# A two-layer hybrid backbone on one core: head 0's keys loaded early, transposes over two PSUM pools, and the last projection as seven block products

## The chip, the cores and the metric

The kernel runs on one core of a Trainium2 chip. Its engines work in parallel, each through its own list of instructions in order: TensorE (PE) multiplies matrices and writes to PSUM, VectorE (DVE) and ScalarE (ACT) work on tiles element by element, GpSimd (POOL) does so more slowly, and SyncE (SP) issues the transfers between HBM and SBUF. They wait for each other by semaphores. The metric is the device time of one execution in microseconds (us), as the median of three runs; lower is better.

## The reference

There are 512 latent tokens x, 256 context tokens and a width of 2048. Layer 1 is even, layer 2 odd; both have adaLN (shift, scale and gate from the conditioning) ahead of them and a gated residual behind. Cut to what matters here:

```python
def even_layer(...):                       # layer 1
    h = modulate(rms_norm(x, norm_g), sh, sc)
    au, av, ag, bq, bk, bv, bg = split(h @ w_in)
    q, k = diff_qk(bq, ...), diff_qk(bk, ...)      # QK-norm and rotary; keys of ctx appended
    ob = blocked_diff_attention(q, k_all, v_all, lam)   # 8 heads, two maps each
    y = even_branch_out(au, av, ag, ob, bg, ...)
    return x + gt * (y @ w_out)

def conv_module(h, w_in, dw_w, dw_b, ln_g, ln_b):   # in layer 2
    a, b, g = jnp.split(h @ w_in, 3, axis=-1)
    y = a * jax.nn.sigmoid(b)
    y = depthwise_conv_31(y) + dw_b
    y = jax.nn.silu(layer_norm(y, ln_g, ln_b))
    return y * jax.nn.silu(g)

def odd_layer(...):
    h = modulate(rms_norm(x, norm_g), sh, sc)
    return x + gt * (conv_module(h, ...) @ w_out)
```

Everything is float32. The last product, `conv_module(...) @ w_out` in layer 2, is 512x2048 by 2048x2048.

## The kernel before

**Arithmetic.** A float32 product is made of three matmuls on parts of reduced width: each operand is split in a rounded part (hi) and the rest (lo), and hi·hi, lo·hi and hi·lo are added up in PSUM. For weights, `load_w` (lines 97 to 105) loads a raw tile of 128 x 2048 elements (four blocks of 128 rows by 512 columns, 1 MB), ACT copies it to `whi` (L103) and DVE or POOL subtracts to get `wlo` (L104). Raw tiles have three buffers, `whi` and `wlo` two each. Activations are split the same way by `split` (L111 on ACT, L112 on DVE).

**Stages.** By the profiled execution's clock: adaLN and the keys of the context to about 140 us; layer 1's input projections and the gated MLP to 648; attention, filled up with the remaining projections, to 970; its output projection and the residual to 1131; h2, layer 2's modulated input, transposed by PE and split, to 1191; layer 2's input projection, in groups of four 128-column tiles with DVE running the 31-tap convolution beside it, to 1673; the last projection to 1847.

**Order.** In the input projections of layer 1 and in attention, PE and SP follow the order of the code (a manual schedule). Elsewhere the scheduler of the tile framework sets each engine's order from its own estimates and from priorities: weight loads and their splits are put 100 places ahead (`W_AHEAD`), the gates' work 600 (`E_AHEAD`). Within an engine the resulting order is fixed: an instruction that waits holds up all behind it.

**The places that the change touches.** `load_kq` (L828 to 835) loads the keys `kk` and queries `qq` of a head from HBM into the attention's pool, which has two buffers for each; head 0 is loaded right at the attention's start, with `S` (the scores) waiting for it. `make_h2` transposes four 128x128 blocks into one PSUM tile of the pool `psM` (two banks, `z4`), from which ACT (L1061) and DVE (L1062) make h2's hi and lo. The other six banks belong to `psA` (`mt`). At the end of layer 2 the chain `ln_chain` normalises the 16 conv tiles `zs` (16 tiles of the pool `rs4`, tag `res`), multiplies by the gates `sg` (pool `sg4`; L1167 makes a gate from its projection `tg`), and `y2_split` makes hi and lo. The chain's pieces are taken between the granules of the last three gate projections, so most of it comes after the mean and variance of all conv tiles are known. The last projection then runs over four groups of 512 columns (`og`) with four loads of 512 rows each (`gi`): a granule is one load and 48 matmuls of 512 columns, into four banks. Its `wlo` is made on POOL. After each group DVE multiplies by the gate (L1244), adds x1 (L1245), and SP writes the output.

## Time and profile before

| | us |
|---|---|
| three runs | 1850.75, 1850.77, 1851.95 |
| median | 1850.77 |
| the profiled execution's own time | 1853.68 |
| its span (first to last instruction) | 1851.9 |
| PE busy | 1805.9 (98%), 8767 instructions |
| DVE busy | 1122.3 (61%) |
| ACT busy | 559.8 (30%) |
| POOL busy | 446.9 (24%) |
| mean granted clock of TensorE | 0.996 |

A row of the profile's groups reads: line, engine, operation, output from inputs, shapes, how many; then busy time and mean ns of one; then the engine's idle time before them and what ended it. A row of the timeline reads: start, duration, engine, line, operation, how many in a row, and in brackets how long the engine had been idle and what released it. A row of the windows: stretch, length, busy time (with instructions) of PE, its weight loads, DVE, ACT and POOL, the granted clock, the DMA engines' busy share and GB/s. A row of the waits: engine, line, what it waited for, total us, times, longest.

### The profile page before, as it was taken

The numbers are of one execution on the slowest core, as the hardware profiler recorded it, in microseconds if no ns is written. First come the engines' busy times: TensorE is split into PE (matmuls) and PEld (weight loads), VectorE is DVE, ScalarE is ACT, GpSimd is POOL, SyncE is SP. The second block draws the span as 40 slices with busy tenths as digits, with TensorE's granted clock in tenths as the row PEclk, the third lists the DMA queues.
The fourth block names the chain that finished last, engine by engine and source line by source line (L and its number), as shares of the span: only waits on it lengthen the run. The fifth ranks groups of instructions, "written<-read, shape, count | busy, mean of one in ns | idle before, by whom it ended". The sixth has DMA issues, their size and how long they took to land.

```text
span 1851.9 us, 21931 instructions
## 1 busy us (share of the span) xinstructions
PE 1805.9 (98%) x8767; PEld 1475.8 (80%) x8767; DVE 1122.3 (61%) x1571; ACT 559.8 (30%) x747; POOL 446.9 (24%) x173
## 2 busy tenths in 40 slices
PE   5899999999999989999999999999999999999998
PEld 2557888888878878888888889888888888888887
DVE  4438546288556336666674555149999999765111
ACT  3322212222323124444442225322222222464120
POOL 0002002011000032232310002245445544444332
PEclk9999999999999999999999999999999999999999
DMA  9997764397767485655656772222332233224441
GB/s 312 360 333 254 245 240 123 118 347 232 241 230 240 165 225 161 170 164 167 203 193 228 250 232 86 91 91 91 102 103 91 91 104 101 91 91 142 149 158 52
DMA packets 208487, 327.34 MB, mean 177 GB/s; under 512 B 10249, under 2 KB 116610, under 8 KB 200194
## 3 DMA queue, kind: packets, MB, share of 16 engines
q1 hardware_dynamic: 208386, 325.94, 54.5%
q8 instruction: 69, 1.13, 0.3%
q14 instruction: 32, 0.26, 0.0%
HBM read 292.33 MB, written 33.58 MB: 176 GB/s over the span
## 4 chain that ended last, share of the span: by engine, by line
PE 83%; DMA 8%; DVE 4%; issue 2%; ACT 1%; POOL 1%; SPq 1%; DVEq 0%; ACTq 0%; POOLq 0%
PE tg L67 31%; PE mb L67 20%; PE m L67 14%; PE fm L67 8%; DMA raw<-in_o_ada_w_dram 3%; PE S L67 2%; PE oT L67 2%; PE z L305 2%; DVE wlo L104 2%; DVE acc L466 1%; DMA raw<-in_e_w_in_dram 1%; PE t L883 1%; DMA qq<-q_s 1%; DMA x_s<-x 1%; POOL wlo L104 1%
## 5 line engine op out<-in xcount | busy, mean ns | idle before, releaser
L104 POOL TENSOR_TENSOR wlo<-raw,whi 128x2048 fp32r<-128x2048 f32 x80 | 369.3, 4617 | 634.1 <-ACT whi L103 626.7
L103 ACT CAST whi<-raw 128x2048 fp32r<-128x2048 f32 x136 | 259.6, 1909 | 697.3 <-PE tg L67 209.7
L1152 DVE SCALAR_TENSOR_TENSOR z<-y,dwc,z 128x512 f32<-128x512 f32 x480 | 319.4, 749 | 0.1
L67 PE MATMUL tg<-h2h,wlo 128*128 128x512 f32 x704 | 274.7, 390 | 0.0
L67 PE MATMUL tg<-h2l,whi 128*128 128x512 f32 x704 | 273.9, 389 | 0.0
L67 PE MATMUL tg<-h2h,whi 128*128 128x512 f32 x704 | 270.8, 389 | 0.0
L67 PE MATMUL mb<-whi,hhi 128*128 128x512 f32 x512 | 203.0, 398 | 1.4 <-DVE ms L193 1.4
L67 PE MATMUL mb<-wlo,hhi 128*128 128x512 f32 x512 | 201.1, 393 | 1.5 <-DVE wlo L104 1.3
L104 DVE TENSOR_TENSOR wlo<-raw,whi 128x2048 fp32r<-128x2048 f32 x56 | 128.2, 2290 | 120.4 <-ACT whi L103 120.1
L67 PE MATMUL mb<-whi,hlo 128*128 128x512 f32 x512 | 200.9, 392 | 0.0
L466 DVE SCALAR_TENSOR_TENSOR acc<-raw,silu_c,acc 128x2048 f32<-128x2048 f32 x60 | 141.0, 2351 | 91.1 <-DMA raw<-in_o_ada_w_dram 70.2
L67 PEld LDWEIGHTS tg<-h2l,whi 128*128 128x128 f32 x704 | 132.2, 188 | 27.8 <-issue 0.5
L67 PEld LDWEIGHTS tg<-h2h,wlo 128*128 128x128 f32 x704 | 132.2, 188 | 27.7 <-issue 0.5
L67 PEld LDWEIGHTS tg<-h2h,whi 128*128 128x128 f32 x704 | 132.2, 188 | 27.5
L194 POOL TENSOR_TENSOR rs<-ms,mhalf 128x8 f32<-128x8 f32 x20 | 35.5, 1784 | 377.8 <-DVE ms L193 377.8
L67 PEld LDWEIGHTS mb<-whi,hhi 128*128 128x128 f32 x512 | 96.5, 189 | 34.6 <-issue 13.5
L67 PEld LDWEIGHTS mb<-wlo,hhi 128*128 128x128 f32 x512 | 96.7, 189 | 21.7 <-DVE wlo L104 2.7
L67 PEld LDWEIGHTS mb<-whi,hlo 128*128 128x128 f32 x512 | 96.6, 189 | 20.3
L67 PE MATMUL fm<-hhi,whi 128*128 128x512 f32 x256 | 106.7, 417 | 0.6 <-DVE mx L711 0.6
L67 PE MATMUL fm<-hlo,whi 128*128 128x512 f32 x256 | 101.1, 395 | 0.0
L67 PE MATMUL fm<-hhi,wlo 128*128 128x512 f32 x256 | 100.8, 394 | 0.0
L67 PE MATMUL m<-wlo,y2h 128*128 128x512 f32 x256 | 99.6, 389 | 0.0
(260 smaller groups left out, 3004.4 us busy)
## 6 DMA issues: line engine op xcount, KB each, us to landing
raw<-in_e_w_in_dram SPq DMA_DIRECT2D x56, 1024.0 KB, 6.4
raw<-in_o_ada_w_dram SPq DMA_DIRECT2D x48, 1024.0 KB, 5.0
raw<-in_o_w_in_dram SPq DMA_DIRECT2D x48, 1024.0 KB, 5.1
raw<-in_e_ada_w_dram SPq DMA_DIRECT2D x64, 512.0 KB, 7.2
raw<-in_e_ada_w_dram SPq DMA_DIRECT2D x16, 1024.0 KB, 6.7
raw<-in_e_w_out_dram SPq DMA_DIRECT2D x16, 1024.0 KB, 5.2
raw<-in_o_w_out_dram SPq DMA_DIRECT2D x16, 1024.0 KB, 5.0
qq<-q_s SPq DMA_DIRECT2D x16, 512.0 KB, 11.9
```

The costliest lines, as they stand in the source:

```text
L67: return PE.matmul(o, l, r, start=start, stop=stop)
L103: A.copy(hi, raw)
L104: (lo_eng or V).tensor_tensor(lo, raw, hi.bitcast(F32), op=ALU.subtract)
L194: G.tensor_tensor(dst, tmp, mhalf[:, 0:1].broadcast_to([P, n]), op=ALU.pow)
L305: PE.matmul(ada_ps[j][32 * g : 32 * g + 32, 0 : 2 * nc_], S[:, kt, :], raw[:, i, :], start=(kt < 4), stop=(kt >= KT - 4), skip_group_check ...
L466: V.scalar_tensor_tensor(ada_state["acc"], raw, sc_[:, jt : jt + 1], ada_state["acc"], op0=ALU.mult, op1=ALU.add)
L883: PE.transpose(z[:, k * P : (k + 1) * P], e[:, (k0 + k) * P : (k0 + k + 1) * P], ident)
L1152: V.scalar_tensor_tensor(zi if t == TAPS - 1 else z, y2[:, t : t + T], w(t), z, op0=ALU.mult, op1=ALU.add)
```

## The change

Three edits.

*Keys of head 0.* `load_kq` moves up, and even heads get a pool of their own, `kq0` with one buffer; odd heads keep one buffer in the attention's pool. Head 0's loads are now issued inside the gated MLP's loop, once its first projection (`ug == 0`) has been issued. On SP, before, the loads stand at the attention's start, behind the last stores `ug_s` of the gated MLP:

```order
L712 DMA ug_s<-mx_4558 128x512
L712 DMA ug_s<-mx_4577 128x512
L95 DMA raw_4807<-in_e_w_in_dram 128x8x256
L712 DMA ug_s<-mx_4596 128x512
L712 DMA ug_s<-mx_4615 128x512
L95 DMA raw_4950<-in_e_w_in_dram 128x8x256
L831 DMA kk_4635<-k_s 64x2x768 x2
L834 DMA qq_4636<-q_s 64x4x512 x2
```

In the changed kernel they stand among the stores of the last queries, some 50 rows earlier:

```order
L565 DMA q_s<-qkhi_3324 128x4x128
L565 DMA q_s<-qklo_3325 128x4x128
L565 DMA q_s<-qkhi_3349 128x4x128
L565 DMA q_s<-qklo_3350 128x4x128
L660 DMA kk_4297<-k_s 64x2x768 x2
L663 DMA qq_4298<-q_s 64x4x512
L565 DMA q_s<-qkhi_3374 128x4x128
L663 DMA qq_4298<-q_s 64x4x512
L95 DMA raw_3622<-in_e_w_in_dram 128x4x512
L565 DMA q_s<-qklo_3375 128x4x128
```

The four transfers (two for `kk`, two for `qq`) now stand ahead of the weight load `raw_3622` and between the last stores of the queries.

*Transposes.* `make_h2` takes its PSUM tile from `psM` and `psA` in turn; `sg4` has 13 tiles instead of 12.

*The last projection.* It is cut in halves of rows (token halves), of the inner dimension and of columns, and done as seven products of blocks with fifteen sums (the form of Strassen's method after Winograd). For each of two halves of 1024 columns (`u`) there are 14 steps, each with one weight tile of 1 MB as before and 24 matmuls into two banks. In order, with g the half of the inner block's 1024 rows: for g = 0 and 1 the steps m1, n5, n6, n4, then m2, m2, then m7, n3, m7, n3. In m1, m2 and n3 the weights are used as loaded and split on POOL. In n5, n6, n4 and m7 DVE first adds two weight tiles in place (`add`, L1326), then ACT copies `whi` (L1303) and DVE subtracts `wlo` (L1304). The activations' sums are made once, in `y2_sums`: for each of eight pairs of tiles four differences of 128x256 (L1258 to 1261, DVE), four roundings (L1266, ACT) and four subtractions (L1267, DVE). The combinations of the products and the results (L1322 to 1324) follow on DVE; a result loads x1 into a `res` tile, adds, and writes out from it.

What this does to DVE's order at the end of layer 2: before, the rows around the last gates' operations L1167 (which read the last projections `tg` and so free their banks) are the layer norm's alone:

```order
L1167 SCALAR_TENSOR_TENSOR sg_1807_12560<-sg_1807_12560,tg_1775_12288 128x512
L1204 TENSOR_TENSOR z4_1765_12214<-z4_1765_12214,sg_1726_11953 128x512
L112 TENSOR_TENSOR y2l_1764_12210<-z4_1762_12205,y2h_1763_12209 128x512
L1167 SCALAR_TENSOR_TENSOR sg_1808_12563<-sg_1808_12563,tg_1776_12289 128x512
L112 TENSOR_TENSOR y2l_1767_12219<-z4_1765_12214,y2h_1766_12218 128x512
L1203 SCALAR_TENSOR_TENSOR z4_1782_12347<-z4_1782_12347,z_1654_11156 128x512
L1204 TENSOR_TENSOR z4_1782_12347<-z4_1782_12347,sg_1771_12276 128x512
L1203 SCALAR_TENSOR_TENSOR z4_1785_12356<-z4_1785_12356,z_1656_11190 128x512
L1167 SCALAR_TENSOR_TENSOR sg_1809_12566<-sg_1809_12566,tg_1777_12290 128x512
```

In the changed kernel the same gates' operations are line 1181, and stand behind the weight splits of the first steps and the first sums:

```order
L1326 TENSOR_TENSOR X0_12737<-X0_12737,X1_12738 128x2048
...
L1304 TENSOR_TENSOR wlo_1859_12759<-X0_12737,whi_1858_12758 128x2048
...
L1326 TENSOR_TENSOR X0_12737<-X0_12737,X2_12739 128x2048
...
L1304 TENSOR_TENSOR wlo_1863_12793<-X0_12737,whi_1862_12792 128x2048
L1260 TENSOR_TENSOR z_1558_9952<-z_1558_9952,z_1559_9953 128x256
L1267 TENSOR_TENSOR sl_1787_12374<-z_1559_9953,y2h_1742_12105 128x256
L1260 TENSOR_TENSOR z_1560_9954<-z_1560_9954,z_1561_9955 128x256
L1267 TENSOR_TENSOR sl_1788_12375<-z_1558_9952,E_1785_12372 128x256
L1181 SCALAR_TENSOR_TENSOR sg_1820_12637<-sg_1820_12637,tg_1775_12300 128x512
L1181 SCALAR_TENSOR_TENSOR sg_1821_12640<-sg_1821_12640,tg_1776_12301 128x512
```

X0 to X3 are the raw weight tiles, `sl` and `E` hold the sums' parts; X0 has three steps' sums added in place, one after the other. The gate operation on `tg_1775` now follows the weight split `wlo_1863` of the third step, n6. On PE the last projection begins, before, with the first granule over four banks:

```order
L67 MATMUL tg_1778_12291<-h2l_1465_8833,whi_1805_12508 128x512
L67 MATMUL m4_1827_12604<-whi_1836_12618,y2h_1742_12101 128x512
L67 MATMUL m4_1828_12605<-whi_1836_12618,y2h_1742_12101 128x512
L67 MATMUL m4_1829_12606<-whi_1836_12618,y2h_1742_12101 128x512
L67 MATMUL m4_1827_12604<-wlo_1837_12619,y2h_1742_12101 128x512
L67 MATMUL m4_1827_12604<-whi_1836_12618,y2l_1743_12102 128x512
```

and in the changed kernel with the step m1 on two banks, after which n5 (on `m4_1864`, the bank of `tg_1775`, and `m4_1865`) and n6 (on `m4_1868` and `m4_1869`) are mixed:

```order
L1315 MATMUL m4_1861_12765<-whi_1856_12752,y2l_1752_12136 128x512
L1313 MATMUL m4_1864_12796<-whi_1858_12758,y2h_1742_12105 128x512
L1314 MATMUL m4_1864_12796<-wlo_1859_12759,y2h_1742_12105 128x512
L1315 MATMUL m4_1864_12796<-whi_1858_12758,sl_1787_12374 128x512
L1313 MATMUL m4_1864_12796<-whi_1858_12758,y2h_1745_12115 128x512
L1314 MATMUL m4_1864_12796<-wlo_1859_12759,y2h_1745_12115 128x512
...
L1313 MATMUL m4_1868_12828<-whi_1862_12792,y2l_1743_12106 128x512
L1314 MATMUL m4_1868_12828<-wlo_1863_12793,y2l_1743_12106 128x512
```

The first five matmuls on `m4_1864` need the sums' part `sl_1787`; the next on it follow after n6 has begun.

The diff; left out are the old loop of the last projection, the bodies of n6 and n4 (which are n5's with other names, banks and signs; n4 adds into `s1`), where the sums `E` lie, the loads `l_` (which call `fetch`), and `bank`, which gives a, b and c two banks of `psA` each and d two of `psM`:

```diff
@@ -647,6 +647,23 @@
+    pkq = p123.enter_context(ExitStack())
+    kq0 = pkq.enter_context(tc.tile_pool(name="kq0", bufs=1))
+    KQ = {}
+
+    def load_kq(h):
+        pool = at if h % 2 else kq0
...
@@ -710,6 +727,8 @@
             V.tensor_tensor(mx, z, gu, op=ALU.mult)
             SP.dma_start(ug_s[g], mx)
+        if ug == 0:
+            load_kq(0)
@@ -927,7 +935,6 @@
         units = [(h, qt) for h in range(H) for qt in range(NT)]
-        load_kq(0)
         load_v(0)
@@ -967,9 +974,10 @@
     psA = ctx.enter_context(tc.tile_pool(name="psA4", bufs=6, space=PSUM))
     rs4 = ctx.enter_context(tc.tile_pool(name="rs4", bufs=16))
-    sg4 = ctx.enter_context(tc.tile_pool(name="sg4", bufs=12))
+    sg4 = ctx.enter_context(tc.tile_pool(name="sg4", bufs=13))
@@ -1045,8 +1053,8 @@
 
     def make_h2(half, kts):
         ts_ = slice(256 * half, 256 * half + 256)
-        for k0 in range(kts[0], kts[1], 2):
-            z = z4()
+        for n, k0 in enumerate(range(kts[0], kts[1], 2)):
+            z = mt() if n % 2 else z4()
             for i in range(2):
                 for u in range(2):
                     kt, t = k0 + i, 2 * half + u
@@ -1143,11 +1151,17 @@
+    ztile = {}
+
     def conv(i, y2):
         z = z4()
         w = lambda t: dwc[:, t * KT + i : t * KT + i + 1]
         V.tensor_scalar(z, y2[:, 0:T], w(0), g2[:, cDB + i : cDB + i + 1], op0=ALU.mult, op1=ALU.add)
-        zi = rs4.tile([P, T], F32, tag="res", name=nm("z"))
+        if i == 0:
+            for k in range(8):
+                for j in (k, k + 8):
+                    ztile[j] = rs4.tile([P, T], F32, tag="res", name=nm("z"))
+        zi = ztile[i]
         for t in range(1, TAPS):
             V.scalar_tensor_tensor(zi if t == TAPS - 1 else z, y2[:, t : t + T], w(t), z, op0=ALU.mult, op1=ALU.add)
         if i == 0:
@@ -1210,10 +1224,48 @@
 
     y2m = [None] * KT
 
+
+    TH = T // 2
+    lo_h, hi_h = slice(0, TH), slice(TH, T)
+    S_ = {}
+
     def y2_split(i, z):
         hi, lo = htile("y2h"), htile("y2l")
-        split(hi, lo, z)
+        r = lo_h if i < 8 else slice(0, T)
+        split(hi[:, r], lo[:, r], z[:, r])
+        A.copy(zs[i], z)
         y2m[i] = (hi, lo)
+        if y2m[(i + 8) % KT]:
+            y2_sums(i % 8)
+
...
+    def y2_sums(k):
+        y1, y2 = zs[k], zs[k + 8]
+        a11, a21, a12, a22 = y1[:, lo_h], y1[:, hi_h], y2[:, lo_h], y2[:, hi_h]
+        V.tensor_tensor(a22, a21, a22, op=ALU.subtract)
+        V.tensor_tensor(a21, a21, a11, op=ALU.subtract)
+        V.tensor_tensor(a11, a11, a22, op=ALU.subtract)
+        V.tensor_tensor(a12, a12, a11, op=ALU.subtract)
+        e3, e4 = e_tiles(k)
+        L = [(rs4 if k else sg4).tile([P, T], F32R, tag="res" if k else "sg", name=nm("sl")) for _ in range(2)]
+        for n, v, hi, lo in ((1, a22, y2m[k][0][:, hi_h], L[0][:, lo_h]), (2, a11, y2m[k][1][:, hi_h], L[0][:, hi_h]),
+                             (3, a21, e3, L[1][:, lo_h]), (4, a12, e4, L[1][:, hi_h])):
+            A.copy(hi, v)
+            V.tensor_tensor(lo, v, hi.bitcast(F32), op=ALU.subtract)
+            S_[n, k] = (hi, lo)
 
     chain = ln_chain()
     for gi in range(1, 4):
@@ -1227,23 +1279,163 @@
             y2_split(i, z)
 
 
-    gt2b = row_tiles(gt2_s, "gt2b")
-    y2stat = [(y2m, t * P) for t in range(NT)]
...
+
+    def quarter(c, h):
+        return [(y2m[8 * c + k][0][:, h], y2m[8 * c + k][1][:, h]) for k in range(8)]
+
+    ops = {"11": quarter(0, lo_h), "12": quarter(1, lo_h), "22": quarter(1, hi_h)}
+    for n in (1, 2, 3, 4):
+        ops[f"s{n}"] = [S_[n, k] for k in range(8)]
+    X = [ap_.tile([P, 4, T], F32, tag="acc", name="X0")]
+    X += [wp.tile([P, 4, T], F32, tag="raw", bufs=3, name=f"X{i}") for i in (1, 2, 3)]
+    sgt = lambda n: sg4.tile([P, T], F32, tag="sg", name=nm(n))
+    s1, qd, u2, gtb = ([sgt(n) for _ in range(2)] for n in ("s1", "qd", "u2", "gtb"))
+
+    def fetch(x, u, i, j, g):
+        r0, c0 = 1024 * i + 512 * g, 1024 * u + 512 * j
+        SP.dma_start(x, o_w_out[r0 : r0 + 512, c0 : c0 + 512].rearrange("(k p) n -> p k n", p=P))
+        return x
+
+    def parts(x, eng):
+        hi = wp.tile([P, 4, T], F32R, tag="whi", name=nm("whi"))
+        lo = wp.tile([P, 4, T], F32R, tag="wlo", name=nm("wlo"))
+        A.copy(hi, x)
+        eng.tensor_tensor(lo, x, hi.bitcast(F32), op=ALU.subtract)
+        return hi, lo
+
+    def product(banks, op, g, w, first, last):
+        hi, lo = w
+        for b in range(2):
+            ts_ = slice(b * P, b * P + P)
+            for k in range(4):
+                ah, al = ops[op][4 * g + k]
+                PE.matmul(banks[b], ah[:, ts_], hi[:, k, :], start=first and g == 0 and k == 0, stop=False, skip_group_check=True)
+                PE.matmul(banks[b], ah[:, ts_], lo[:, k, :], start=False, stop=False, skip_group_check=True)
+                PE.matmul(banks[b], al[:, ts_], hi[:, k, :], start=False, stop=last and g == 1 and k == 3, skip_group_check=True)
+
+    def result(u, i, j, b, ps):
+        xr = rs4.tile([P, T], F32, tag="res", name=nm("xr"))
+        rows = slice((2 * i + b) * P, (2 * i + b + 1) * P)
+        cs = slice(1024 * u + 512 * j, 1024 * u + 512 * j + 512)
+        SP.dma_start(xr, x1_s[rows, cs])
+        V.tensor_tensor(ps, ps, gtb[j], op=ALU.mult)
+        V.tensor_tensor(xr, ps, xr, op=ALU.add)
+        SP.dma_start(out[rows, cs], xr)
+
+    add = lambda x, y: V.tensor_tensor(x, x, y, op=ALU.add)
+    two = range(2)
+    steps = []
+    for u in range(2):
+
+        order = ((0, 1, 2, 3), (1, 2, 3, 0))
...
+        for g in two:
+            r, t1, t2, t3 = order[g]
+
+            def m1(g=g, r=r, bank=bank):
+                w = parts(X[r], G)
+                yield
+                product(bank("a"), "11", g, w, True, True)
+                if g:
+                    for b in two:
+                        A.copy(s1[b], bank("a")[b])
+
+            def n5(g=g, r=r, t1=t1, bank=bank):
+                add(X[r], X[t1])
+                w = parts(X[r], V)
+                yield
+                product(bank("c"), "s1", g, w, True, True)
+                if g:
+                    for b in two:
+                        V.tensor_tensor(qd[b], bank("c")[b], s1[b], op=ALU.subtract)
+
...
+            steps.append(([l_(0, r, 0, 0, g)], m1))
+            steps.append(([l_(1, t1, 0, 1, g)], n5))
+            steps.append(([l_(2, t2, 1, 1, g)], n6))
+            steps.append(([l_(3, t3, 1, 0, g)], n4))
+        for g in two:
+            def m2(g=g, u=u, bank=bank):
+                w = parts(X[2 + g], G)
+                yield
+                product(bank("a"), "12", g, w, False, True)
+                if g:
+                    for b in two:
+                        result(u, 0, 0, b, bank("a")[b])
+
+            steps.append(([l_(0, 2 + g, 1, 0, g)], m2))
+        for g in two:
+            def m7(g=g, u=u, bank=bank):
+                add(X[2 * g], X[2 * g + 1])
+                w = parts(X[2 * g], V)
+                yield
+                product(bank("b"), "s3", g, w, False, True)
+                if g:
+                    for b in two:
+                        d = bank("d")[b]
+                        V.tensor_tensor(d, bank("b")[b], qd[b], op=ALU.add)
+                        result(u, 1, 1, b, d)
+                        V.tensor_tensor(bank("b")[b], s1[b], bank("b")[b], op=ALU.subtract)
+                        result(u, 1, 0, b, bank("b")[b])
+
+            def n3(g=g, u=u, bank=bank):
+                w = parts(X[2 * g + 1], G)
+                yield
+                product(bank("c"), "s4", g, w, False, True)
+                if g:
+                    for b in two:
+                        add(bank("c")[b], u2[b])
+                        result(u, 0, 1, b, bank("c")[b])
+
+            steps.append(([l_(0, 2 * g, 0, 1, g), l_(1, 2 * g + 1, 1, 1, g)], m7))
+            steps.append(([], n3))
+
+    gens = [f() for _, f in steps]
+    NSTEP = len(steps)
+    for n in range(NSTEP + 3):
+        if n < NSTEP:
+            for f in steps[n][0]:
+                f()
+        if 0 <= n - 2 < NSTEP:
+            with tc.high_priority(offset=W_AHEAD):
+                next(gens[n - 2])
+        m = n - 3
+        if m >= 0:
+            if m % 14 == 0:
+                for j in two:
+                    c0 = 1024 * (m // 14) + 512 * j
+                    SP.dma_start(gtb[j], gt2_s[c0 : c0 + 512].partition_broadcast(P))
+            next(gens[m], None)
```

More of the change, by code (lines that the diff above doesn't have):

```diff
@@ L647, in hybrid_layers_kernel @@
     p12a.close()
+    pkq = p123.enter_context(ExitStack())
[3 more added lines that the diff above has]
+        pool = at if h % 2 else kq0
+        kk = pool.tile([P, 2, TA], F32R, tag="kk", bufs=1, name=nm("kk"))
+        qq = pool.tile([P, 4, T], F32R, tag="qq", bufs=1, name=nm("qq"))
+        for s in range(2):
+            ds_ = slice(DH * s, DH * s + DH)
+            SP.dma_start(kk[ds_].bitcast(F32), k_s[h, s].rearrange("(m d) t -> d m t", d=DH))
+        for s in range(2):
+            ds_ = slice(DH * s, DH * s + DH)
+            SP.dma_start(qq[ds_].bitcast(F32), q_s[h].rearrange("s (m d) t -> d (s m) t", d=DH))
+        KQ[h] = ([kk[:, m, :] for m in range(2)], [[qq[:, 2 * s + m, :] for s in range(2)] for m in range(2)])
     p12b = p12.enter_context(ExitStack())
@@ L822, in fill @@
             n -= 1
-    KQ, VV, S0, OT, PP = {}, {}, {}, {}, {}
-    def load_kq(h):
-        kk = at.tile([P, 2, TA], F32R, tag="kk", bufs=2, name=nm("kk"))
-        qq = at.tile([P, 4, T], F32R, tag="qq", bufs=2, name=nm("qq"))
-        for s in range(2):
-            ds_ = slice(DH * s, DH * s + DH)
-            SP.dma_start(kk[ds_].bitcast(F32), k_s[h, s].rearrange("(m d) t -> d m t", d=DH))
-        for s in range(2):
-            ds_ = slice(DH * s, DH * s + DH)
-            SP.dma_start(qq[ds_].bitcast(F32), q_s[h].rearrange("s (m d) t -> d (s m) t", d=DH))
-        KQ[h] = ([kk[:, m, :] for m in range(2)], [[qq[:, 2 * s + m, :] for s in range(2)] for m in range(2)])
+    VV, S0, OT, PP = {}, {}, {}, {}
     def load_v(h):
@@ L969, in hybrid_layers_kernel @@
     p3.close()
+    pkq.close()
     psA = ctx.enter_context(tc.tile_pool(name="psA4", bufs=6, space=PSUM))
     rs4 = ctx.enter_context(tc.tile_pool(name="rs4", bufs=16))
-    sg4 = ctx.enter_context(tc.tile_pool(name="sg4", bufs=12))
+    sg4 = ctx.enter_context(tc.tile_pool(name="sg4", bufs=13))
     t4 = ctx.enter_context(tc.tile_pool(name="t4", bufs=2))
```

51 lines of the change are left out of this document (36 added, 15 removed).

## The prediction

> **What bounds the kernel now.** The profiled execution took 1853.68 us with a span of 1851.9; the runs' median, 1850.77, is 2.9 us lower. I read the shares first.
>
> ```profile
> PE 1805.9 (98%) x8767; PEld 1475.8 (80%) x8767; DVE 1122.3 (61%) x1571; ACT 559.8 (30%) x747; POOL 446.9 (24%) x173
> ```
>
> PE is the bound on average, so fewer matmuls should pay. Averages hide stages, so next the end of the chain of waits (start, us, what), then the two stretches of the last stage by windows (PE, PEld, DVE, ACT, POOL busy; clock; DMA share; GB/s).
>
> ```profile
> 1191.42 405.96 PE tg L67 x1791
> ...
> 1635.00 37.90 PE tg L67 x167
> 1672.90 174.09 PE m L67 x768
> ```
>
> ```profile
> 1644.70:1672.90 28.20, 28.20 (x126) 23.38 (x125) 20.08 (x32) 20.28 (x30) 12.41 (x3) 1.00 0.33 108
> 1672.90:1847.20 174.30, 174.08 (x768) 143.86 (x767) 37.10 (x52) 36.45 (x29) 69.13 (x15) 1.00 0.38 126
> ```
>
> The last projection is 768 matmuls in 174.09, or 0.2267 us each at full clock, with DVE nearly free. Just ahead of it DVE is busy 20.08 of 28.20: that is the layer norm's end. The change puts its new work at that seam. The waits that the other two parts aim at:
>
> ```profile
> PE S L67 <- DMA qq<-q_s: 3.7, 1, 3.7
> ...
> PE m L67 <- ACT h2h L1061: 0.5, 1, 0.5
> ```
>
> **Part 1, head 0's keys (-6.5).** PE around the attention's start, the clock of that stretch, the two loads on SP and the load's landing in the chain:
>
> ```profile
> 668.50 0.39 PE L67 MATMUL fm<-hlo,whi 128*128 128x512 f32 x1
> 672.63 2.90 PE L67 MATMUL S<-kk,qq 128*128 128x256 f32 x8 [3.75 <-DMA qq<-q_s]
> 675.33 0.63 PE L67 MATMUL fm<-hhi,whi 128*128 128x512 f32 x1
> 675.76 0.63 PE L67 MATMUL fm<-hhi,wlo 128*128 128x512 f32 x1
> ...
> 680.31 0.40 PE L67 MATMUL fm<-hhi,whi 128*128 128x512 f32 x1
> 680.54 0.39 PE L67 MATMUL fm<-hhi,wlo 128*128 128x512 f32 x1
> ```
>
> ```profile
> 672.60:690.00 17.40, 17.37 (x71) 14.40 (x72) 8.50 (x13) 8.19 (x13) 4.61 (x1) 0.83 0.74 177
> ```
>
> ```profile
> 657.84 1.32 SPq L831 DMA_DIRECT2D kk<-k_s  x2
> 659.20 1.86 SPq L834 DMA_DIRECT2D qq<-q_s  x2
> ```
>
> PE idles 3.75. The matmuls behind it start 0.43 apart where later ones start 0.23 apart: eight of them cost 1.6, and the eight score matmuls about 1.5 (2.90 against half). Loaded 190 us earlier, all of 6.8 goes; I take 6.5, ends 3 and 8. The Trainium skill ("TensorE: Matmul & The Clock Gate", the HAM clock gate) says an idle PE drops to a lower clock; the 0.43 spacing agrees. Next late would be the values and head 1's keys, but fill matmuls stand between.
>
> The loads move to about 470, ahead of a weight load on SP:
>
> ```profile
> 470.00:480.00 10.00, 10.00 (x52) 7.35 (x51) 3.71 (x4) 2.18 (x4) 0.00 (x0) 1.00 0.78 228
> 480.00:490.00 10.00, 10.00 (x50) 8.37 (x49) 3.64 (x4) 1.91 (x1) 0.00 (x0) 1.00 0.43 110
> ```
>
> By the shapes (two of 64x2x768 and two of 64x4x512, four bytes each) that is 1.8 MB more where the queues are 0.78 and then 0.43 busy. At the 228 GB/s of 0.78 it takes 8 us, part of it in free time. The cover is the raw tiles that are already loaded, each 48 matmuls or 10.9 us of PE. I cost it at 0; -2 to +4 with the cover short.
>
> **Part 2, transposes (0).** The whole wait on a transposed tile is the 0.5 quoted above, so 0, ends -1 and +1.5.
>
> **Part 3, Strassen: gain -21.8.** Two column halves of 14 steps with 24 matmuls are 672 instead of 768: 96 x 0.2267. A step is 24 x 0.2267 = 5.44 us of PE. What feeds a step:
>
> ```profile
> L104 POOL TENSOR_TENSOR wlo<-raw,whi 128x2048 fp32r<-128x2048 f32 x80 | 369.3, 4617 | 634.1 <-ACT whi L103 626.7
> L103 ACT CAST whi<-raw 128x2048 fp32r<-128x2048 f32 x136 | 259.6, 1909 | 697.3 <-PE tg L67 209.7
> ...
> L104 DVE TENSOR_TENSOR wlo<-raw,whi 128x2048 fp32r<-128x2048 f32 x56 | 128.2, 2290 | 120.4 <-ACT whi L103 120.1
> L466 DVE SCALAR_TENSOR_TENSOR acc<-raw,silu_c,acc 128x2048 f32<-128x2048 f32 x60 | 141.0, 2351 | 91.1 <-DMA raw<-in_o_ada_w_dram 70.2
> ```
>
> *Steady chain (+14.9).* In n5, n6, n4 and m7 the weights are summed in place (2.35, by L466's row, the nearest: two 128x2048 inputs), copied by ACT (1.91) and subtracted by DVE (2.29): 6.55 in series, since the next sum overwrites what the subtraction reads. That is 1.11 more than 5.44. The second half has eight such steps, 8.9; a pair of POOL steps adds some 0.8, because the copy waits for PE to release one of two whi buffers and 1.91 + 4.61 = 6.52 follow: 9.7. The last eight steps of the first half have four, 4.4 + 0.8 = 5.2. Lower end 5, if neighbouring POOL steps build up a lead; upper 20.
>
> *Head (+29).* DVE is the queue to follow. Its unit times: 0.60 for a 512-wide operation in a row of them, 0.34 for a 256-wide one (two started 0.67 ahead of the next); I use 0.61 with handoffs.
>
> ```profile
> 1639.83 4.87 DVE L1195 TENSOR_TENSOR z<-z,z 128x512 f32<-128x512 f32 x8
> ...
> 462.75 0.76 DVE L549 TENSOR_TENSOR rot<-tn,SG 128x256 f32<-128x256 f32 x2
> 463.42 0.69 DVE L112 TENSOR_TENSOR qklo<-z,qkhi 128x512 fp32r<-128x512 f32 x1
> ```
>
> ```profile
> 1664.09 4.64 POOL L104 TENSOR_TENSOR wlo<-raw,whi 128x2048 fp32r<-128x2048 f32 x1 [6.26 <-ACT whi L103]
> ...
> 1685.85 4.61 POOL L104 TENSOR_TENSOR wlo<-raw,whi 128x2048 fp32r<-128x2048 f32 x1 [5.81 <-ACT whi L103]
> ```
>
> The first sum X0+=X1 overwrites what POOL reads for m1, so it starts at 1664.09 + 4.64 = 1668.7. From it to the gate operation that frees n5's first bank (the change's DVE rows shown above) stand two sums and two subtractions (9.3), eleven 512-wide operations (6.7) and eight 256-wide (2.7), with 1.3 of waiting for a whi buffer held to 1672.9: 1688.7, against 1678.3 when PE is free. Then, down to the second group's n5, come three large operations (7.0), 17 of 512 (10.4) and 56 of 256 (19.0): 1725.1, and n5's subtraction ends at 1727.4. Ideally that step starts after five, at 1672.9 + 27.2 = 1700.1. So 27.3 late on DVE's work alone. POOL adds to it:
>
> ```profile
> 1683.88 0.70 DVE L1226 TENSOR_TENSOR z<-z,sg 128x512 f32<-128x512 f32 x1
> ...
> 1687.48 4.13 DVE L1226 TENSOR_TENSOR z<-z,sg 128x512 f32<-128x512 f32 x2
> 1691.66 1.30 DVE L112 TENSOR_TENSOR y2l<-z,y2h 128x512 fp32r<-128x512 f32 x2
> ```
>
> The two L1226, 0.70 alone, ended only after POOL did at 1690.46. A POOL subtraction for m1's second group falls among the sums and can hold them up to 4.6, making 31.9. I take 29; ends 20 and 36. The Trainium skill ("SBUF — State Buffer", who interferes with whom) says a DVE operation with two SBUF inputs is locked out while GpSimd reads; the trace agrees, and by the rule the head would be 31.9 instead of 27.3.
>
> *Middle (+7).* Between the halves the `res` pool has two free tiles, since the summed operands hold 14 of 16. So eight results pass through two tiles: output write, then the next load of x1, each time, with DVE standing in order at the addition and n5's and n6's subtractions behind it. The landings, min, median, max, of xr's loads and then of the outputs:
>
> ```profile
> L1238 SPq DMA_DIRECT2D xr<-x_s x16: 319/430/490, 1671.4 to 1805.8; - x16
> ...
> DMA to landing us min/median/max: 3.0/4.8/6.3
> ```
>
> ```profile
> L1246 SPq DMA_DIRECT2D out_dram<-ot x16: 332/356/458, 1709.7 to 1848.5; - x16
> ...
> DMA to landing us min/median/max: 2.3/4.4/7.6
> ```
>
> From m7's end M: four combinations and an addition, M+3.1; out and in 9.2 with 0.4 of issue, M+12.7; its second tile M+15.2, and n5's subtraction ends at M+17.5. The last pair of results passes at M+25.6 and n6's subtraction ends at M+27.9; n6 was due at about M+16.3, and 3 to 5 of the lateness are already in the steady term. So 7; by the minima 2, by the maxima 16.
>
> *Tail (+2.4)* and *clock (+1).* Before, the last matmul is followed by a multiplication and an addition:
>
> ```profile
> 1847.01 0.70 DVE L1244 TENSOR_TENSOR m<-m,gt2b 128x512 f32<-128x512 f32 x1 [1.29 <-PE m L67]
> 1847.75 0.69 DVE L1245 TENSOR_TENSOR ot<-m,xr 128x512 f32<-128x512 f32 x1
> ```
>
> Now m7's results queue ahead of n3's, which have one operation more: four more of 0.6. After the head's stalls of 10 us a few matmuls run at 0.43: 1 (0 to 4).
>
> **Sum.** -21.8 - 6.5 + 0 + 0 + 14.9 + 29 + 7 + 2.4 + 1 = +26.0. Against the profiled execution: span 1877.9, time 1879.7. Against the median: **1877 us**, 1.4% slower.
>
> **Rivals.** *A, the gain is kept (1823).* The mechanism: the sums are done under the g projection, PE stays fed and 28.3 - 1 is realised. For it: 98% PE, and 8 us of idle DVE between 1644.7 and 1672.9. Against it: the normalised tiles appear only after 1644.7, and 36.4 us of DVE work stands behind 1688.7. It decides if the second group's n5 starts by about 1703, since the other losses, 25.3, leave 3 of the 28.3. 6%.
> *B, half of it is hidden.* The head covered and the chain not: -28.3 + 14.9 + 7 + 3.4 = -3.0, 1848. The chain and middle covered and the head not: -28.3 + 29 + 3.4 = +4.1, 1855. For it: POOL steps need no DVE and give DVE time to run ahead. Against it: only two whi and two wlo buffers, so no lead beyond two steps. 10%.
> *C, worse (1896).* SP's queue holds weight loads behind result loads, and each POOL subtraction locks DVE's chains: the middle 16, the steady chain 20, the head 34, giving +45. For it: L1226's 4.13; against it, DMA is only 0.38 busy. 10%.
> *D, part 1 does nothing*, the values being late next: +6.5, 1883, inside my range; part of the 74% for the forecast.
>
> **Numbers.** The forecast, 74%, has its own range 1864 to 1890 from the terms' ends. With C and part of B the range is 1855 to 1895. A change under 0.2%, 3.7 us, cannot be told from none. Faster: A and four of B, 10%; same: five of B, 5%; slower 85%.
>
> **What would show it.** After: 672 matmuls in the last stage, PE idle there by some 50 us, over half of it ahead of the second group's n5 (the sixth step), with releasers DVE wlo, the gate operation or the sums' lo parts; n5 of the second group at 1727 to 1732 less 6.5; a second idle stretch at the halves' seam behind xr loads; no wait of S on qq. The forecast is wrong if PE's idle time in the last stage is under 20 us, or if h2's or the attention's stage moves by over 5.

## The result and the profile after

The changed kernel takes 1883.49 us (median of 1881.46, 1883.49 and 1884.06) against 1850.77 before: a ratio of 1.0166, with a 95% interval of 1.0145 to 1.0187. The profiled execution took 1884.06 with a span of 1882.3. The forecast was 1877, slower by 1.4%; it is slower by 1.7%.

The page's shares of the changed kernel:

```profile
PE 1797.3 (95%) x8671; PEld 1461.2 (78%) x8671; DVE 1227.7 (65%) x1691; ACT 602.7 (32%) x811; POOL 430.1 (23%) x169
```

PE has 96 instructions less and is 8.6 us less busy, where 96 matmuls at 0.2267 would have been 21.8: part of what is left runs at a lower clock. To see where the time went, the two kernels are cut at the first matmul of each stage. The views are those of tiles (instruction, how many, min/median/max ns, first and last start) and of the timeline; first the kernel before:

```profile
L67 PE MATMUL fm<-hhi,whi x256: 387/396/792, 652.3 to 936.9; 128*128 128x512 f32 x128
...
L67 PE MATMUL m<-whi,yh x256: 278/389/496, 977.0 to 1135.8; 128*128 128x512 f32 x96, 128*128 128x256 f32 x32
...
L67 PE MATMUL tg<-h2h,whi x704: 389/389/476, 1191.3 to 1672.1; 128*128 128x512 f32 x176
...
1672.74 0.84 PE L67 MATMUL m<-whi,y2h 128*128 128x512 f32 x3
```

and the changed kernel:

```profile
L67 PE MATMUL fm<-hhi,whi x256: 387/396/792, 651.5 to 929.4; 128*128 128x512 f32 x128
...
L67 PE MATMUL m<-whi,yh x256: 277/389/497, 969.4 to 1129.5; 128*128 128x512 f32 x96, 128*128 128x256 f32 x32
...
L67 PE MATMUL tg<-h2h,whi x704: 389/389/478, 1180.0 to 1660.8; 128*128 128x512 f32 x176
...
1661.45 0.39 PE L1313 MATMUL m<-whi,y2h 128*128 128x512 f32 x1
```

| stage, from first matmul to first matmul (us) | before | after | difference | forecast |
|---|---|---|---|---|
| to the attention's first fill matmul (fm) | 652.3 | 651.5 | -0.8 | 0 |
| attention, to layer 1's output projection (m) | 324.7 | 317.9 | -6.8 | -6.5 |
| output projection and h2, to layer 2's input (tg) | 214.3 | 210.6 | -3.7 | 0 |
| layer 2's input projection | 481.4 | 481.4 | 0 | 0 |
| last projection, to the end | 179.2 | 220.9 | +41.7 | +32.5 |
| span | 1851.9 | 1882.3 | +30.4 | +26.0 |

The last projection's waits of PE (line, what it waited for, total us, times, longest), of which there were none before:

```profile
PE m L1313 <- DVE sg L1181: 10.2, 1, 10.2
PE m L1314 <- POOL wlo L1304: 7.2, 7, 2.4
PE m L1314 <- DVE wlo L1304: 7.2, 6, 1.7
PE z L1313 <- ACT z L1237: 6.9, 1, 6.9
PE m L1313 <- ACT whi L1303: 6.5, 3, 3.3
PE m L1313 <- DVE xr L1323: 3.9, 2, 2.0
PE m L1315 <- DVE sl L1267: 2.0, 2, 1.8
```

That is 43.9 us in all. The same stage in four stretches of the windows: the first five steps (120 matmuls), the rest of the first half (nine steps), the seam between the halves (three steps), the last eleven steps and the end. A boundary matmul may count in both.

```profile
1661.45:1718.55 57.10, 34.64 (x121) 26.23 (x120) 54.58 (x97) 35.22 (x64) 4.76 (x1) 0.79 0.28 102
1718.55:1776.25 57.70, 51.21 (x217) 40.07 (x216) 34.25 (x31) 17.75 (x10) 22.76 (x5) 1.00 0.58 194
1776.25:1803.85 27.60, 20.64 (x73) 15.56 (x72) 17.44 (x12) 5.72 (x3) 0.27 (x1) 0.81 0.74 234
1803.85:1882.30 78.45, 64.22 (x265) 49.95 (x263) 41.08 (x38) 20.15 (x12) 24.14 (x5) 0.97 0.42 143
```

At 5.44 a step these would be 27.2, 49.0, 16.3 and 59.8 plus some 5 for the end. In the first stretch DVE is busy 54.58 of 57.10: the engine that had 37 us of work in the whole stage before is now its bound. The head row by row, DVE and POOL of the changed kernel:

```profile
1672.94 2.28 DVE L1304 TENSOR_TENSOR wlo<-X,whi 128x2048 fp32r<-128x2048 f32 x1
...
1676.48 2.47 DVE L1181 SCALAR_TENSOR_TENSOR sg<-sg,tg 128x512 f32<-128x512 f32 x4
...
1698.76 4.76 POOL L1304 TENSOR_TENSOR wlo<-X,whi 128x2048 fp32r<-128x2048 f32 x1 [41.33 <-ACT whi L1303]
1699.07 4.73 DVE L1260 TENSOR_TENSOR z<-z,z 128x256 f32<-128x256 f32 x1
1703.72 0.41 DVE L1258 TENSOR_TENSOR z<-z,z 128x256 f32<-128x256 f32 x1
...
1718.21 2.29 DVE L1304 TENSOR_TENSOR wlo<-X,whi 128x2048 fp32r<-128x2048 f32 x1 [0.69 <-ACT whi L1303]
```

The third step's weight split stands ahead of the gate operations, as in the order shown with the change; the first of these ends at 1677.2, and PE's first matmul of n5 starts there (1677.21, after 10.2 of waiting; of the five matmuls shown with the change, only the third reads `sl`). The sum L1260 takes 4.73 where the next operation of that size takes 0.41, for as long as POOL subtracts. This also holds up PE in the fourth step: n4 needs a bank that a normalised tile still occupies, ACT copies that tile only after DVE has finished with it, and DVE comes to it behind the L1260 of 4.73:

```profile
1705.70 0.59 ACT L1237 COPY z<-z 128x512 f32<-128x512 f32 x1 [0.34 <-DVE y2l L112]
1706.34 0.80 PE L1313 MATMUL z<-whi,y2h 128*128 128x512 f32 x1 [6.93 <-ACT z L1237]
```

The second group's n5 has its weights at 1720.5, 59 us after the stage's start.

### The profile page after: what moved, and what is told of

Same layout as the page of the kernel before. It is cut to its first block, busy times and chain, and to the rows that moved or that the text cites. A ratio compares the mean times of both kernels' runs of the same rounds, so it can differ in the third digit from the quotient of the medians.

```text
span 1882.3 us, 21962 instructions
## 1 busy us (share of the span) xinstructions
PE 1797.3 (95%) x8671; PEld 1461.2 (78%) x8671; DVE 1227.7 (65%) x1691; ACT 602.7 (32%) x811; POOL 430.1 (23%) x169
## 4 chain that ended last, share of the span: by engine, by line
PE 75%; DMA 8%; DVE 8%; issue 4%; POOL 3%; ACT 2%; SPq 0%; POOLq 0%; DVEq 0%; ACTq 0%
PE tg L67 30%; PE mb L67 18%; PE fm L67 8%; PE m L67 7%; DMA raw<-in_o_ada_w_dram 4%; PE S L67 2%; POOL wlo L1304 2%; PE oT L67 2%; PE z L305 2%; DVE wlo L104 1%; DVE acc L466 1%; ACT whi L1303 1%; DVE wlo L1304 1%; PE t L891 1%; PE m L1314 1%
## 5 line engine op out<-in xcount | busy, mean ns | idle before, releaser
L103 ACT CAST whi<-raw 128x2048 fp32r<-128x2048 f32 x120 | 229.2, 1910 | 596.5 <-PE tg L67 208.8
L104 POOL TENSOR_TENSOR wlo<-raw,whi 128x2048 fp32r<-128x2048 f32 x64 | 295.7, 4620 | 522.1 <-ACT whi L103 516.2
L1304 POOL TENSOR_TENSOR wlo<-X,whi 128x2048 fp32r<-128x2048 f32 x12 | 56.5, 4712 | 167.6 <-ACT whi L1303 167.6
```

The costliest lines, as they stand in the source:

```text
L103: A.copy(hi, raw)
L104: (lo_eng or V).tensor_tensor(lo, raw, hi.bitcast(F32), op=ALU.subtract)
L1304: eng.tensor_tensor(lo, x, hi.bitcast(F32), op=ALU.subtract)
```

## Experiments

Each is compared with the kernel before on the same chip. Since the start of the attention differs from run to run (its first fill matmul stood at 647.6 to 652.3 in the profiles of the two kernels and of those with the small parts alone), the length of a stage in the profile tells more than the time where a few us matter.

### Parts 1 and 2 without part 3, and each alone

The edits are the hunks of the diff above that belong to the parts: `load_kq` and `kq0` for part 1; `mt() if n % 2 else z4()` and `sg4`'s 13 tiles for part 2.

> Parts 1 and 2 of the change, the last projection as before. In the changed kernel the last projection's first matmul stands at 1661.45 us instead of 1672.74, so 11.3 us are gained ahead of it. If that gain is the two small parts', this kernel takes 1850.8 - 11.3 = 1839.5 and its last stage is the old 174 us. If some of it comes from the other order that the last projection brings with it (weight loads, gates), it is between 1840 and 1848.

> Part 1 alone. My theory (idle 3.75 and the slow clock after it, 6.5 to 7.5 in the changed kernel's trace between the first fill matmul and the output projection): 1843.3 to 1844.3, no wait of S on qq, granted clock 1.00 instead of 0.91 between 640 and 680. Rival: only the idle itself goes, 3.75, and 1847.

> Part 2 alone. My prediction's step: 0, between -1 and +1.5, so 1850 to 1852. Rival, from the changed kernel's trace, in which h2's stage is 3.7 us shorter: two more banks let PE run through the transposes and the three short waits on wlo and h2h (2.7 in sum) go, 1847.

Measured: both parts 1842.2, ratio 0.9948 (0.9929 to 0.9967); part 1 alone 1846.5, 0.9961 (0.9947 to 0.9975); part 2 alone 1850.5, 0.9984 (0.9974 to 0.9993), where the kernel before had a median of 1853.1 on that chip. So part 1 is worth 6.6 and part 2 some 2.6 in time. Both together are worth 10.9 of the 11.3 that the changed kernel gains ahead of its last stage, and the last stage is as long as before: that gain is the two small parts'.

By stages: with part 1 alone the attention takes 318.0 instead of 324.7, and PE's waits around its start hold no transfer any more. The rival (only the idle time goes) would have been 3.75, so the slow matmuls after it go too: the granted clock from 640 to 680 is 1.00 instead of 0.91. With both parts, the output projection and h2 take 209.9, against 215.2 with part 1 alone. PE's waits in that stretch, first with part 1 alone, then with both:

```profile
PE m L67 <- DVE wlo L104: 3.8, 3, 1.6
...
```

```profile
PE m L67 <- DVE wlo L104: 0.5, 1, 0.5
```

Three waits on weight splits shrink to one; they are not waits on transposed tiles, but they stand among the transposes. 3.3 of the 5.4 are these waits, and 0.5 is the one on a transposed tile. Why two more banks shorten them is not shown by any run. Part 2 alone has one wait of 2.6 on a weight split there, and its stretch is only 0.6 shorter than before: by the profiles its worth lies between 0.6 and 5.4.

One more kernel has parts 1 and 2, but 12 tiles in `sg4` as before:

```diff
-    sg4 = ctx.enter_context(tc.tile_pool(name="sg4", bufs=13))
+    sg4 = ctx.enter_context(tc.tile_pool(name="sg4", bufs=12))
```

> Parts 1 and 2 without the thirteenth gate tile: the keys' own pool and the transposes in both PSUM pools, with the old last projection. If the tile does nothing there, the time is that of the kernel with the parts 1 and 2 whole, 1842, with h2's stage as short as there (209.9 us from the first matmul of layer 1's output projection to the first of layer 2's gates and conv inputs). Rival: the thirteenth tile is what shortens it, and the time is that of part 1 alone, 1846.5.

Measured: 1842.63, ratio 0.9942 (0.9928 to 0.9956); the stretch takes 211.5. In all profiles of the study it takes 209.7 to 213.6 in the twelve kernels with part 2, and 214.2 and 215.2 in the two without. The tile is not what helps. These two kernels, the changed one without its third part, are the fastest of the study, below both the kernel before and the changed one.

### The parts of the head and the chain

In the kernels of this and the next section the stage starts at nearly the same place, so marks are counted from its first matmul: after 144 matmuls (the start of the seventh step), after 336 (the second half) and after 408 (its fourth step). Where neighbouring steps are mixed, a mark goes by the count; filler matmuls are not counted.

| us | to the 7th step | to the second half | three steps of the seam | rest | whole stage |
|---|---|---|---|---|---|
| at 5.44 a step | 32.7 | 43.5 | 16.3 | 59.8 and the end | |
| changed kernel | 64.2 | 50.6 | 27.6 | 78.5 | 220.9 |
| no activation sums | 49.2 | 49.6 | 19.9 | 75.4 | 194.1 |
| no weight sums | 57.6 | 47.1 | 25.5 | 71.1 | 201.3 |
| four result tiles | 64.4 | 50.6 | 23.7 | 75.9 | 214.6 |
| PE kept busy | 65.5 | 49.6 | 26.8 | 78.4 | 220.2 |
| second half's splits on DVE | 64.7 | 49.7 | 23.5 | 75.1 | 213.0 |
| four result tiles and second half's splits on DVE | 65.3 | 51.9 | 24.1 | 71.6 | 212.9 |

**No activation sums.**

```diff
-        V.tensor_tensor(a22, a21, a22, op=ALU.subtract)
...
-            A.copy(hi, v)
-            V.tensor_tensor(lo, v, hi.bitcast(F32), op=ALU.subtract)
-            S_[n, k] = (hi, lo)
+        for n in (1, 2, 3, 4):
+            S_[n, k] = (y2m[k][0][:, lo_h], y2m[k][1][:, lo_h])
```

> The changed kernel without the activations' sums: their four differences, roundings and subtractions for each of eight pairs are left out, and the products take other tiles in their place; matmuls, weight sums and results are as before. My theory: the 64 DVE operations of 0.34 stand ahead of the second group's n5, and with them goes the 4.3 us that one of them was held by POOL; that step then starts 40 us after m1 instead of 59, and the time is 1883.5 - 19 = 1864, or 4 to 6 lower where the clock stays up. Rival: the head is the chain of weight sums and the gates' late release of banks, and 1878 or more is left.

Measured: 1856.5, ratio 1.0018 (1.0007 to 1.0029), so 27 us of the changed kernel's time are gone, more than expected. To the sixth step it took 40.1 instead of 57.1 us. That is 17 of the 19 expected, and the rival falls. In this kernel PE waits in the stage as follows; the waits on sg, on sl and on z's copy are gone:

```profile
PE m L1305 <- POOL wlo L1295: 9.8, 7, 3.9
PE m L1304 <- ACT whi L1294: 7.9, 4, 2.9
PE m L1305 <- DVE wlo L1295: 7.4, 6, 1.6
...
```

The other part was not foreseen: the seam is 7.7 shorter. Without the sums their tiles in `res` stay free, so the results are not short of tiles. This kernel therefore also speaks on the seam.

**No weight sums.**

```diff
             def n5(g=g, r=r, t1=t1, bank=bank):
-                add(X[r], X[t1])
                 w = parts(X[r], V)
```

and so in n6, n4 and m7.

> The changed kernel without the sums of weight tiles: the 16 additions of two 128x2048 tiles are left out, and the products use the first tile alone; the activations' sums, matmuls and results are as before. My theory: the chain addition, copy, subtraction falls from 6.55 to 4.2 and under a step's 5.44, so PE's waits on DVE wlo (7.2 in all) go; ahead of the second group's n5 three additions of 2.3 go as well, 7; the waits on POOL wlo (7.2) stay. Together some 15: 1868. Rival: two buffers of whi and wlo set the pace in every step, whichever engine subtracts, so the waits on wlo stay near 14 and only the head's 7 go: 1876.

Measured: 1864.2, ratio 1.0058 (1.0035 to 1.0080); the stage is 19.6 shorter, more than the 15 expected. PE's waits in its stage:

```profile
PE m L1313 <- DVE sg L1181: 7.8, 1, 7.8
...
PE m L1314 <- POOL wlo L1304: 5.6, 7, 1.2
...
PE m L1314 <- DVE wlo L1304: 1.4, 1, 1.4
```

The waits on DVE's wlo fall from 7.2 in six places to 1.4 in one, as the chain's theory wants (1.91 + 2.29 fits in 5.44, 6.55 does not), and those on POOL's stay in all seven. The head gives 6.6, the rest of the first half 3.5, the last eleven steps 7.4. The rival, that two buffers set the pace whoever subtracts, fits the POOL steps alone, and their waits fall too, from 7.2 to 5.6.

### Seam, clock and POOL

**Four result tiles.**

```diff
-        xr = rs4.tile([P, T], F32, tag="res", name=nm("xr"))
+        xr = (sg4 if b else rs4).tile([P, T], F32, tag="sg" if b else "res", name=nm("xr"))
```

> The changed kernel with half of the results' tiles taken from the gates' pool, so that four tiles instead of two carry the first half's results. My theory for the seam between the halves: PE's two waits on DVE xr (3.9), the wlo wait behind them and the half-speed matmuls after them (3.3 in the ten us from 1791) go, 6 to 8: 1876. Rival: the seam's time is DVE's order and the transfers' landing whatever the tiles: 1883.

Measured: 1877.1, ratio 1.0123 (1.0102 to 1.0144); the stage is 6.3 shorter. At the seam the changed kernel's PE, and DVE where it matters:

```profile
1781.13 0.69 DVE L1323 TENSOR_TENSOR xr<-m,xr 128x512 f32<-128x512 f32 x1 [0.57 <-DMA xr<-x_s]
1781.74 2.28 DVE L1304 TENSOR_TENSOR wlo<-X,whi 128x2048 fp32r<-128x2048 f32 x1
...
1784.07 0.51 PE L1314 MATMUL m<-wlo,y2h 128*128 128x512 f32 x1 [1.70 <-DVE wlo L1304]
...
1791.18 0.47 PE L1313 MATMUL m<-whi,y2l 128*128 128x512 f32 x1 [1.83 <-DVE xr L1323]
1793.68 0.79 PE L1313 MATMUL m<-whi,y2l 128*128 128x512 f32 x1 [2.03 <-DVE xr L1323]
1795.88 0.80 PE L1314 MATMUL m<-wlo,y2l 128*128 128x512 f32 x1 [1.40 <-DVE wlo L1304]
1796.47 0.63 PE L1315 MATMUL m<-whi,sl 128*128 128x512 f32 x1
```

A weight split stands behind an addition that waits for a load, PE stands behind both, and then runs at half its rate. With four tiles the seam's one wait is this:

```profile
PE m L1314 <- DVE wlo L1304: 4.8, 1, 4.8
```

So the waits on results are gone, but DVE is still late for n5. Of the seam's 11.3 above its steps 3.9 went.

**PE kept busy.**

```diff
+    zw = cp.tile([P, 64], F32, tag="zw", name="zw")
+    V.tensor_scalar(zw, ident[:, 0:64], 0.0, None, op0=ALU.mult)
...
+                if u == 0 and g == 0:
+                    for _ in range(15):
+                        PE.matmul(bank("a")[0][0:64, 0:480], zw, dwc[:, 0:480], start=False, stop=False, ...)
                 product(bank("c"), "s1", g, w, True, True)
```

> The changed kernel with 15 matmuls of a zero weight tile, which add zero to m1's first bank, between m1 and n5, so that PE works through the 10.2 us of its first wait. The trace of the changed kernel has 16.5 us of matmuls that start more than 0.227 apart in the last stage, 4.4 of them in the 20 us after that wait. If this slow clock is on the path, those go to near 0 and the time falls by 4: 1879. Rival: DVE's queue sets the head whatever the clock, the waits on sl grow by what the matmuls save, and the time stays within 1 of 1883.5.

Measured: 1884.8, ratio 1.0164 (1.0139 to 1.0188), the stage 0.6 shorter. The rival holds: the ratio is that of the changed kernel (1.0166). The stage's first 19 us have a clock of 1.00, where the changed kernel's same stretch has 0.79:

```profile
1660.88:1680.00 19.12, 19.12 (x61) 9.51 (x60) 17.70 (x25) 12.87 (x22) 0.00 (x0) 1.00 0.37 135
```

```profile
1661.45:1680.57 19.12, 8.96 (x33) 7.00 (x32) 17.68 (x25) 12.87 (x22) 0.00 (x0) 0.79 0.37 135
```

DVE's busy time in it is the same, 17.70 and 17.68, and the seventh step starts no earlier, at 65.5. The fillers outlast the wait they fill, so that n5 starts 17.8 us after the stage's start instead of 15.8; after 48 matmuls both kernels stand at 24.6. Where DVE sets the pace here, neither PE's clock nor these 2 us cost anything.

**Second half's splits on DVE.**

```diff
-                w = parts(X[r], G)
+                w = parts(X[r], V if u else G)
```

and so in m2 and n3.

> The changed kernel with the second half's six POOL subtractions moved to DVE (2.29 instead of 4.6). My theory: a POOL step needs 1.91 + 4.61 after a whi buffer is released, 1.1 more than a step's 5.44; on DVE 4.2 fit, and nothing holds the port. Four of the seven waits on POOL wlo lie in the second half, 4 us: 1879.5. Rival: DVE has the sums' chain to carry, and six more operations of 2.3 in its order make waits on DVE wlo grow by as much: 1883.5.

Measured: 1873.9, ratio 1.0111 (1.0092 to 1.0131). The stage is 7.9 shorter, 4.1 of it at the seam and 3.4 behind; the remaining difference of the times lies ahead of the stage, which the edit doesn't touch. The waits on POOL in the second half are gone and those on DVE's wlo are no more than before (4.1 + 0.5 for 4.9):

```profile
PE m L1314 <- DVE wlo L1304: 4.1, 2, 2.3
...
PE z L1314 <- DVE wlo L1304: 0.5, 1, 0.5
```

More than the four us expected came of it. What a POOL step costs beside its wait is seen in the changed kernel at the second half's m2:

```profile
1838.20 2.29 DVE L1326 TENSOR_TENSOR X<-X,X 128x2048 f32<-128x2048 f32 x1 [2.80 <-DMA X<-in_o_w_out_dram]
1839.19 5.73 POOL L1304 TENSOR_TENSOR wlo<-X,whi 128x2048 fp32r<-128x2048 f32 x1 [3.08 <-ACT whi L1303]
```

```profile
1844.97 0.50 PE L1314 MATMUL m<-wlo,y2h 128*128 128x512 f32 x1 [2.37 <-POOL wlo L1304]
...
1846.47 0.63 PE L1314 MATMUL m<-wlo,y2h 128*128 128x512 f32 x1
1846.89 0.63 PE L1315 MATMUL m<-whi,y2l 128*128 128x512 f32 x1
...
1849.87 0.40 PE L1314 MATMUL m<-wlo,y2h 128*128 128x512 f32 x1
```

An addition of DVE had begun first, POOL's subtraction took 5.73 instead of 4.6, PE waited 2.37, and eight matmuls after it ran at half rate, another 1.6.

**Both together.** The edits are this one and the four result tiles.

> The changed kernel's own order of steps, with four result tiles and the second half's splits on DVE. Alone they gave 6.4 and 9.6 (in the last stage 6.3 and 7.9). If the new order of steps was what spoiled the kernel with all three (1878.6), these two add up to 14 in the last stage: 1868 to 1870. Rival: both work at the same place, the seam and the second half, where DVE now has more to do, and they overlap: 1873 or more.

Measured: 1875.4, ratio 1.0112 (1.0098 to 1.0126), the stage 7.9 shorter, not 14. The table shows the overlap: the seam is 24.1, as with either edit alone (23.7 and 23.5). The last eleven steps gain 6.9, against 2.6 and 3.4 alone, but the two stretches ahead of the seam lose 2.4.

### Another order of the steps

The steps of each half are put in the order m1, m1, m2, m2, n5, n6, n4, n5, n6, n4, m7, n3, m7, n3, with the weight tiles dealt out anew and m2's results after n4:

```diff
-        order = ((0, 1, 2, 3), (1, 2, 3, 0))
...
+        st([(0, 0, 0, 0)], m1, 0, Y[0])
+        st([(1, 0, 0, 1)], m1, 1, Y[1])
+        st([(2, 1, 0, 0)], m2, 0, Y[2])
+        st([(3, 1, 0, 1)], m2, 1, Y[3])
+        st([(1, 0, 1, 0)], nsum, 0, Y[0], Y[1], "c", "s1")
...
```

> The changed kernel with another order of the steps in each half: m1, m1, m2, m2, then n5, n6, n4 twice, then m7, n3, m7, n3. The first four steps need no summed activations. My theory of the head: DVE's work sets the start of the second group's n5, some 59 us after m1's start, and now seven steps instead of five lie ahead of it, so the head's wait falls by up to two products, 10.9, and the time to 1874. Rival: m2 needs tiles 8 to 15 of y2, which the same DVE queue makes, so the wait only moves to m2, and three chained sums follow each other without a POOL step between the groups: 1883 or more.

Measured: 1878.0, ratio 1.0135 (1.0103 to 1.0167); the stage 212.9, or 8.0 shorter. By the count, the eighth step, now the second group's n5, starts 68.0 us after the first matmul. That is 29.9 later than after seven unhindered steps, and the changed kernel's sixth step was 29.9 later than after five. So the waits ahead of it moved and did not fall, as the rival said: the fourth step starts at 32.0 where three unhindered steps take 16.3. The theory's 10 in the head is refuted. Half of the stage takes 114.1 instead of 114.8; the three steps that follow take 17.7 instead of 27.6, and the rest 81.1 instead of 78.5. The gain lies at the seam, and no run tells which part of the new order brings it. The two largest of PE's waits in the stage are now on ACT's copies, 13.2 where the changed kernel has 6.5, and on POOL's splits, 8.5 for 7.2:

```profile
PE m L1313 <- ACT whi L1303: 13.2, 6, 6.9
PE m L1314 <- POOL wlo L1304: 8.5, 8, 2.8
...
```

All three edits at once (this order, four tiles, the second half's splits on DVE):

> The last order of steps (m1, m1, m2, m2 first), four result tiles and the second half's splits on DVE together. The last two alone gave 1877.1 and 1873.9 from 1883.5, 6.4 and 9.6. If they lie at different places they add up: 1867 with the new order at no gain, 1857 with its gain of 10. Rival: with more on DVE the second half is bound by its queue and the gains overlap: 1872 or more. In each case it is above the 1842 of the kernel that has parts 1 and 2 alone.

Measured: 1878.6, ratio 1.0130 (1.0106 to 1.0155), the stage 216.1: the rival. No version in this study that makes all sums of the seven products comes below 1873; even the two that leave sums out, at 1856.5 and 1864.2, are not below the kernel before.

## Why the prediction held, and where it was off

**Right, with its mechanism.** The forecast was slower by 26 and it is 32.7 by the medians, inside the range. PE's idle time in the last stage was foreseen at some 50 us and is 43.9, 22.5 of it ahead of the second group's n5. DVE's wlo, a gate operation and the sums' lo parts were named as releasers and are there; ACT's copies, 13.4 together and 10.3 of them ahead of the second group's n5, were not named. That the total came so near is in part luck: by the profiles the last stage was 9.2 us slower than foreseen (41.7 for 32.5) and what lies ahead of it 4.8 faster (11.3 for 6.5).

- *The gain:* 96 matmuls less, and where PE doesn't wait it keeps 5.44 a step. Nothing else was gained.
- *Part 1:* 6.5 foreseen; 6.8 in the attention's stage and 6.6 alone. The moved loads cost nothing that can be told from the spread of the runs.
- *The head:* n5's first bank was foreseen free 15.8 after the stage's start (1688.7 - 1672.9); PE's n5 started 15.76 after it, behind the same two sums, two subtractions, eleven 512-wide and eight 256-wide operations that were counted. The second group's n5 was foreseen 54.5 after it on DVE's work and up to 4.6 more with POOL's hold; it got its weights at 59.05, so the whole of the bound was due: 31.9 by the weights, 29.9 by the matmuls' count, for 29. Without the sums 17 of it go, without the weight sums 6.6. The Trainium skill ("SBUF — State Buffer", who interferes with whom) says that the engine that issues first has the shared ports for the whole instruction and the other blocks. Both directions are here: the sum L1260 at 4.73 instead of 0.41, and POOL's 5.73 beside an addition that had begun a microsecond earlier.
- *The middle:* 7 foreseen, next to some 3 of the steady chain at the same place; the three steps took 11.3 more than 16.3. Four tiles take 3.9 of it away; without the activations' sums, which also frees 14 `res` tiles, 7.7 go.
- *The steady chain* of the steps whose split is on DVE: with the weight sums left out, the waits on DVE's wlo fall from 7.2 to 1.4. Outside the head that kernel's stage is 13.0 shorter, for 14.9. The sum of two weight tiles took 2.29, for the 2.35 of the nearest row.

**Off in size.** Terms that stood against each other, and a sign that contradicts the sum.

- *Part 2 at 0.* The step read the one wait on a transposed tile, 0.5, and took it as all that the part could win. The stage became 3.7 shorter in the changed kernel, and the time 2.6 with part 2 alone. The waits on weight splits in the same stretch fell from 2.8 in the kernel before to 1.2; the step had looked for the tile's name and not for the stretch.
- *The steady chain at 14.9, and the clock at 1.* Behind the head, the three stretches of the table were foreseen at 43.5 + some 5, 16.3 + 10 and 59.8 + some 7 with the end's 7 or 8; they took 50.6, 27.6 and 78.5: 2, 1 and 4 more. The term that was too small is the POOL pair's 0.8, 1.6 in both halves: PE waited on POOL's wlo seven times, 7.2 in all, and at the second half's m2 POOL itself was held by a DVE addition. Moving the second half's six to DVE gave 7.9. The clock failed in its rule: it counted stalls of 10 us alone, while half-rate matmuls follow waits of 2 us as well. By the timeline, the matmuls of the stage that start late without a wait make 14.1 us (16.5 in the expectation of that experiment), 6.6 of them in the first five steps. There most of them cost nothing: with PE kept busy the first 36 us of the stage run at full clock, and it gains 0.6. The other 7.5 are part of those 2, 1 and 4.
- *The tail at 2.4.* From the start of the last matmul to the end it took 6.6 us instead of 5.3, so 1.3.
- *The sign at the attention.* The prediction called itself wrong if the attention's stage moved by over 5. It moved by 6.8, but the prediction's own sum puts 6.5 there: the sign was badly drawn, not the step wrong.

**Rivals.** A needed the second group's n5 within 30 us of the stage's start; it came at 59. B's two halves are ruled out by the same runs, since head and chain each cost what was foreseen. C's mechanism, POOL and DVE holding each other's chains, is there in the rows (4.73 and 5.73), though not in C's size. Taking POOL out of the second half gave 7.9, against the 9.2 by which the stage missed its forecast; that all of it comes from this holding is not shown. D fell with part 1's run.

## What to carry to other kernels

An algorithm that trades matmuls for additions is paid on the engine that adds, and at the place where its inputs come into being: the shares of the whole program (DVE 61%) said nothing, the 28 us ahead of the stage (DVE busy 20) said much. Count what stands in that engine's order between the last input and the first product, and look at what the smaller step does to two-deep buffers: a step of 10.9 us hid a preparation of 6.5 us, a step of 5.44 did not. When one change has several parts, run the parts: here two of them are worth 0.5% and the third costs 2.2%, more than four times that.
